# Splitting weight parts three ahead of their product instead of four, in a float32 hybrid decoder layer

## The chip, the cores and the metric

One core of one Trainium2 chip runs the whole program. The metric is device time in microseconds (us) from the start to the end of one execution; lower is better. The time of before is the median of three runs.

## What is computed

One decoder layer over 1024 positions of width 1024, in float32. Cut to what matters here:

```python
def reference(x, norm1_g, w_in, conv_w, conv_norm_g, ret_norm_g, w_out,
              norm2_g, w_up, w_down, final_norm_g):
    h = x
    h = h + hybrid_mixer(rms_norm(h, norm1_g), w_in, conv_w, conv_norm_g, ret_norm_g, w_out)
    h = h + sq_relu_mlp(rms_norm(h, norm2_g), w_up, w_down)
    return rms_norm(h, final_norm_g)

def hybrid_mixer(u, w_in, conv_w, conv_norm_g, ret_norm_g, w_out):
    z = u @ w_in                      # 1024 x 3584, columns for conv and retention
    ...                               # short convolution; chunkwise retention, 4 heads
    return jnp.concatenate([y_conv, y_ret], axis=-1) @ w_out

def sq_relu_mlp(u, w_up, w_down):
    hdn = jax.nn.relu(u @ w_up)       # 1024 x 4096
    return (hdn * hdn) @ w_down
```

## The kernel before

**Products.** Each float32 matrix is used as a sum of two fp32r parts, a rounded one and the rest, and a product is three matmul passes: high by high, high by low, low by high. The input projection, the output projection and the MLP run on TensorE (PE) in products of 12 matmuls (128x128 weights, 512 moving columns) or, in `tile_in` (L520), in pieces of 24. Many of the products are those of a seven-product (Strassen-like) scheme, numbered 1 to 7; their left sides are sums of weight blocks.

**Splitting a weight part.** `split_piece` (L168) takes one 128x512 block of weights that a DMA has brought into a tile `r`. ScalarE (ACT) copies it to `wh`, which rounds it; VectorE (DVE), or GpSimd (POOL) in the mixer when the planner finds it freer, subtracts to give `wl`. `wh` and `wl` have four buffers each (pool `wp`, L108). In the seven-product scheme `Left.split` (L209) also issues POOL operations on the raw blocks (`r<-r,r`, three of them after the part of product 2, one after that of product 5) and, for four of the seven, one DMA that fetches a later block.

**Order of the work.** Nothing reorders instructions: each engine executes its own in the order in which the program emits them, and SyncE (SP) issues the DMAs in that order as well. The list `plan` holds all splits in the order of their products. `prepare()` (L180) takes the next from the list, emits it, and appends the part to `parts`, from which a product pops its weights. How many parts are ahead is therefore settled by how often `prepare` was called before the first product: L297 and L381 call it for two parts each, and then each product pops one and calls it once. Before the output projection a planner (`background`, L428) chooses, from costs it keeps per engine, where the elementwise tasks of convolution, gates and norms go between the products. From the output projection on, the order is written out by hand.

**The stages.** (1) Head: x is loaded, scaled and split; the value projection. (2) `tile_in` pieces and `pair_in` (L824), with retention and convolution beside them. (3) Tiles 22 and 23 (`IN_END`), which use each weight part twice, for the left and the right half of the positions (L910 to L926). (4) The output projection: `group` (L1060), four groups of eight steps; steps 0 to 3 pop a part each, steps 4 to 7 use these again for the right half and call `prepare`. After its matmuls a step with c = 1 reads the bank out: a DVE add into `x` and an ACT square (`out_evac`, L995). Then the steps of `todo` follow. (5) The MLP. Its first 14 products (`for at, ...`, L1251) and then seven cycles of 28 (L1332 to L1348) have one body:

```python
            bk = pairs[x].product(y)      # or down_product
            prepare()
            for f in todo.pop(0):         # splits of activations, V; sums on POOL
                f()
            put_now()
            pairs[x].take(y, bk)          # DVE (or ACT) reads the bank
```

In a cycle, `up` products (into two banks, pool `pu`) alternate with `down` products (four banks, two for each). `take` reads a bank with one to three DVE operations (`t<-t,b`), `down_take` (L1280) with two or four (`x<-x,b`). Activations are split in `v_split` (L1192): ACT copy, then a subtraction `V<-t,V` on DVE or, for j = 1 of most products, on POOL; `v_next` (L1201) forms sums on POOL (`t<-t,t`). Tiles of `x2` that were put aside in DRAM are fetched back at the steps at = 3 and 4 (`fetch_back`, L1034, `x<-k`) and combined on POOL from at = 7 on (`new_basis`, L1004, the first `x<-x,x`). (6) The last stage multiplies what the last 512 hidden columns give (`last_mm`, L1382), with weights `wd` that `last_piece` (L1106) splits, and normalises and stores the result.

Products of the MLP are counted here from the first, product 0 (at = 0); the first cycle begins with product 14.

Of the kernel before, what the change touches and what calls it, by code (L numbers as in the profile page):

```python
# [40 lines left out]
IN_END = [22, 23]  # L41
# [38 lines left out]
def hybrid_layer(  # L80
# [51 lines left out]
    def bank(pool_=None):  # L132
        return (pool_ or pm).tile([P, H], F32, tag="b", name=nm("b"))
# [46 lines left out]
    def prepare(n=1):  # L180
        for _ in range(n):
            if plan:
                part = plan.pop(0)()
                if part is None:
                    part = plan.pop(0)()
                parts.append(part)
# [191 lines left out]
                dve.tensor_scalar_mul(to[:, h, :], src, perhead[:, i, h : h + 1])  # L378

    once = [token_norms]  # L380
    prepare(2)  # L381

    R2 = ssq

# [12 lines left out]
    def mm(piece, banks, rhs, start, stop, ks=range(4)):  # L397

        hi, lo = piece
        ops = [(a, r, k) for k in ks for a, r in ((hi, 0), (hi, 1), (lo, 0))]  # L400
        for i, (a, r, k) in enumerate(ops):
            for n, b in enumerate(banks):
                nc.tensor.matmul(  # L403
                    b, a[:, k, :], rhs(n, k)[r],
                    start=(start and i == 0), stop=(stop and i == len(ops) - 1),
                )
# [15 lines left out]
    def spawn(gen, ready=None, late=0.0):  # L422
        Task(gen, now[0] if ready is None else ready, late).go()
# [36 lines left out]
    def slot():  # L460
        now[0] += SLOT

    def force(key):
        while key not in got:
            background(1e9)
            assert key in got, key
# [36 lines left out]
    def tick(look=LOOK):  # L503
        n = -1
        while n != len(procs):
            n = len(procs)
            background(look)
            norms()
# [227 lines left out]
    def use(f, half, out, z, psum):  # L736

        if f >= 20:
            return gate(f - 20, half, z, out, psum)
        if f % 3 == 1:  # L740
            return conv_h(f // 3, half, z, psum)
        return conv_b(f // 3, half, z, out, psum)
# [168 lines left out]
    for half in range(2):  # L911
        for f, (z, banks, pieces) in ends.items():
            for c in range(2):
                if half == 0:
                    pieces.append(parts.pop(0))
                mm(
                    pieces[c], [banks[half]],
                    lambda n, k: (uh[4 * c + k][:, hs[half]], ul[4 * c + k][:, hs[half]]),
                    c == 0, c == 1,
                )  # L920
                slot()
                if half:
                    prepare()
                if c:
                    spawn(use(f, half, z, banks[half], True), clock[dve])
                tick()  # L926
# [68 lines left out]
    def out_evac(i, half, b):  # L995
        x, g = scaled(i, half)
        dve.tensor_add(x, x, b)
        square_into(sums_[half], x, i == 0)
        if i < 4:
            if un[i] is None:  # L1000
                un[i] = unit(s="un")
            act.activation(un[i][:, hs[half]], x, AF.Copy, scale=g)
# [57 lines left out]
    def group(j):  # L1060
        a, b = j, 4 + j
        ws, banks = {}, {}
        steps = [(a, 0, 0), (b, 0, 0), (a, 1, 0), (b, 1, 0), (a, 0, 1), (b, 0, 1), (a, 1, 1), (b, 1, 1)]
        for s, (i, c, half) in enumerate(steps):
            if half == 0:
                ws[i, c] = parts.pop(0)
            elif j == 0:
                for idx in range(4 * c, 4 * c + 4):
                    force(("split", idx, 1))
            if c == 0:  # L1070
                banks[i, half] = bank((pm, pr)[i == b])
            mm(
                ws[i, c], [banks[i, half]],
                lambda n, k: (y_h[4 * c + k][:, hs[half]], y_l[4 * c + k][:, hs[half]]),
                c == 0, c == 1,
            )
            slot()
            if half:
                prepare()
            if c:  # L1080
                out_evac(i, half, banks[i, half])
            for t in todo.get(8 * j + s, []):
                t()
            if s == 2 and j in (1, 2):
                down.fetch(4)
            tick()
# [8 lines left out]
    for j in range(4):  # L1095
        group(j)
# [467 lines left out]
```

## Time and profile before

| | |
|---|---|
| median of the three runs | 1070.92 us (1070.82 to 1071.99) |
| profiled execution | 1070.03 us, of which the span in the trace is 1068.1 us |
| PE busy | 1054.8 us (99%), 4860 matmuls |
| DVE / ACT / POOL busy | 870.8 (82%) / 463.6 (43%) / 561.6 us (53%) |
| chain that ended last | PE 90%, DVE 6%, ACT 2% |
| granted TensorE clock | 0.999 of full speed |

The 1.9 us between the span and the execution's own time lie around the span. In the timeline a row gives start, duration, engine, line and operation, the tiles written and read, how many instructions were merged, and in brackets the idle time of the engine before it and what ended it. A matmul row's duration is longer than the pitch of matmuls, since they overlap. L74 is the line of the helper through which all elementwise operations are emitted, so tiles tell them apart. A releaser is the one that came last by the profile; where it had long been done it was another.

### The profile page before, as it was taken

Reading aid. Unit: us, or ns where it says so; the run is one execution under the profiler, and the core shown is the slowest. Engines: PE = TensorE matmul, PEld = TensorE weight load, DVE = VectorE, ACT = ScalarE, POOL = GpSimd, SP = SyncE. Lnnn points to the kernel's source line nnn. Section 1 sums busy time; section 2 is a strip of 40 time slices with the busy share of each in tenths; the row PEclk is TensorE's granted clock in tenths of the full one; section 3 lists DMA queues with packets and bytes.
Section 4 is the critical chain, followed back from the end, with each engine's and each line's share of the span. In section 5 each row is a group of like instructions: output and inputs, shape, how many; then the busy total and the mean of one; then the engine's idle time right before and its main releaser. Section 6 shows DMA issues by size and latency. Waiting matters only on the chain.

```text
span 1068.1 us, 13853 instructions
## 1 busy us (share of the span) xinstructions
PE 1054.8 (99%) x4860; PEld 879.2 (82%) x4860; DVE 870.8 (82%) x1231; ACT 463.6 (43%) x906; POOL 561.6 (53%) x381
## 2 busy tenths in 40 slices
PE   9999999999999999999999999999999999999997
PEld 8888888788888888788788888888888888888886
DVE  7446546799998665799999989999899899899955
ACT  8211445673437444443343433343443434334453
POOL 6334324367854233559458267277186295384552
PEclk9999999999999999999999999999999999999999
DMA  7121122122223733051221211211301201200204
GB/s 276 65 58 42 38 80 70 63 95 80 69 69 129 256 115 123 11 187 39 61 59 49 79 31 50 90 30 50 99 21 50 89 21 49 90 21 19 69 30 158
DMA packets 39685, 82.25 MB, mean 77 GB/s; under 512 B 4544, under 2 KB 5696, under 8 KB 39616
## 3 DMA queue, kind: packets, MB, share of 16 engines
q1 hardware_dynamic: 39328, 80.85, 23.5%
q8 instruction: 38, 0.62, 0.2%
q10 hardware_dynamic: 288, 0.52, 0.1%
q14 instruction: 31, 0.25, 0.1%
HBM read 71.92 MB, written 9.44 MB: 76 GB/s over the span
## 4 chain that ended last, share of the span: by engine, by line
PE 90%; DVE 6%; ACT 2%; issue 1%; POOL 1%; DVEq 0%; ACTq 0%; POOLq 0%
PE b L403 55%; PE b L1277 23%; PE b L357 4%; PE b L1386 4%; DVE t L74 1%; DVE wl L74 1%; DVE x L74 1%; DVE m L74 1%; ACT h L74 1%; DVE q L74 1%; DVE V L74 1%; PE b L339 0%; PE b L595 0%; PE b L1436 0%; PE b L246 0%
## 5 line engine op out<-in xcount | busy, mean ns | idle before, releaser
L74 ACT CAST wh<-r 128x512 fp32r<-128x512 f32 x286 | 176.6, 620 | 326.4 <-PE b L403 134.4
L403 PE MATMUL b<-U,wh 128*128 128x512 f32 x1024 | 315.8, 390 | 2.0 <-DVE x L74 1.2
L74 DVE TENSOR_TENSOR wl<-r,wh 128x512 fp32r<-128x512 f32 x250 | 232.8, 933 | 89.0 <-ACT wh L74 87.8
L74 POOL TENSOR_TENSOR r<-r,r 128x512 f32<-128x512 f32 x136 | 210.2, 1548 | 114.1 <-DVE wl L74 66.1
L1277 PE MATMUL b<-V,wh 128*128 128x512 f32 x784 | 242.0, 389 | 0.7 <-POOL V L74 0.4
L403 PEld LDWEIGHTS b<-U,wh 128*128 128x128 f32 x1024 | 191.7, 188 | 43.2 <-issue 2.4
L74 DVE TENSOR_TENSOR x<-x,b 128x512 f32<-128x512 f32 (+1 forms) x312 | 195.5, 673 | 28.8 <-PE b L1386 14.3
L403 PE MATMUL b<-U,wl 128*128 128x512 f32 x512 | 199.2, 389 | 0.0
L1277 PEld LDWEIGHTS b<-V,wh 128*128 128x128 f32 x784 | 147.1, 188 | 32.4 <-POOL V L74 0.9
L74 POOL TENSOR_TENSOR t<-t,t 128x512 f32<-128x512 f32 x70 | 106.3, 1523 | 96.4 <-ACT t L74 50.4
L1277 PE MATMUL b<-V,wl 128*128 128x512 f32 x392 | 152.5, 389 | 0.0
L74 POOL TENSOR_TENSOR wl<-r,wh 128x512 fp32r<-128x512 f32 x36 | 51.4, 1432 | 119.3 <-ACT wh L74 116.5
L403 PEld LDWEIGHTS b<-U,wl 128*128 128x128 f32 x512 | 96.1, 188 | 19.9
L403 PE MATMUL b<-uh,wh 128*128 128x512 f32 x304 | 102.3, 396 | 0.0
L403 PE MATMUL b<-ul,wh 128*128 128x512 f32 x304 | 100.5, 390 | 0.0
L403 PE MATMUL b<-uh,wl 128*128 128x512 f32 x304 | 100.2, 389 | 0.0
L1277 PEld LDWEIGHTS b<-V,wl 128*128 128x128 f32 x392 | 73.6, 188 | 15.2
L74 POOL TENSOR_TENSOR V<-t,V 128x512 fp32r<-128x512 f32 x35 | 49.6, 1418 | 67.0 <-ACT V L74 67.0
L74 DVE TENSOR_TENSOR t<-t,b 128x512 f32<-128x512 f32 x112 | 75.8, 677 | 1.7 <-POOL t L74 1.2
L74 ACT ACTIVATE t<-t 128x512 f32<-128x512 f32 x64 | 40.2, 631 | 81.2 <-DVE t L74 80.5
L74 DVE TENSOR_TENSOR V<-t,V 128x512 fp32r<-128x512 f32 x63 | 70.3, 1116 | 0.0
L403 PEld LDWEIGHTS b<-uh,wl 128*128 128x128 f32 x304 | 57.0, 188 | 12.3
(177 smaller groups left out, 1431.3 us busy)
## 6 DMA issues: line engine op xcount, KB each, us to landing
r<-w_up_t SPq DMA_DIRECT2D x64, 256.0 KB, 2.6
r<-w_down_t SPq DMA_DIRECT2D x56, 256.0 KB, 2.7
r<-w_in_t SPq DMA_DIRECT2D x48, 256.0 KB, 2.7
xt<-xT SPq DMA_DIRECT2D x16, 256.0 KB, 5.4
xs<-xT SPq DMA_DIRECT2D x8, 512.0 KB, 5.0
r<-w_out_t SPq DMA_DIRECT2D x16, 256.0 KB, 2.7
x<-xT SPq DMA_DIRECT2D x8, 512.0 KB, 7.9
k<-x SPq DMA_DIRECT2D x6, 512.0 KB, 3.0
```

What stands on the lines that cost most here:

```text
L74: return f(out, *args, **kw)
L357: nc.tensor.matmul(vb[i], a[k][:, i * P : (i + 1) * P], b[k // 2][:, vs], start=(k == 0 and a is uh and b is vh), stop=(k == KT - 1 and a ...
L403: nc.tensor.matmul(b, a[:, k, :], rhs(n, k)[r], start=(start and i == 0), stop=(stop and i == len(ops) - 1),)
L1277: nc.tensor.matmul(b, a, r, start=(i == 0), stop=(i == len(ops) - 1))
L1386: nc.tensor.matmul(z, a, b, start=(k == 0 and t == 0), stop=(k == 3 and t == 2))
```

## The change

The second `prepare` of the head takes one part instead of two. In the tiles 22 and 23, which called `prepare` four times while their parts were used for the second time, it is called once after the first product and then three times; in each group of the output projection it is called after step 0 and after steps 4, 5 and 6 instead of 4, 5, 6 and 7. Otherwise each `prepare` stays where it is.

```diff
     once = [token_norms]
-    prepare(2)
+    prepare()
...
                 slot()
-                if half:
+
+                if (f, c) == (IN_END[0], 0) if half == 0 else (f, c) != (IN_END[-1], 1):
                     prepare()
...
             slot()
-            if half:
+            if s == 0 or half and s < 7:
                 prepare()
```

No other line differs, and the MLP's own calls are not touched.

## Rows read from the trace of the kernel before

**Rows 1.** Page, busy time of each engine (share of the span, instructions).

```profile
PE 1054.8 (99%) x4860; PEld 879.2 (82%) x4860; DVE 870.8 (82%) x1231; ACT 463.6 (43%) x906; POOL 561.6 (53%) x381
```

**Rows 2.** Waits of PE: total us, times, longest us; two of seven.

```profile
PE b L663 <- ACT h L74: 2.3, 5, 0.7
...
PE b L403 <- DVE x L74: 1.2, 2, 0.7
```

**Rows 3.** Timeline of PE, single rows.

```profile
436.31 0.70 PE L403 MATMUL b<-U,wh 128*128 128x512 f32 x2 [0.70 <-DVE x L74]
...
508.37 0.61 PE L403 MATMUL b<-U,wh 128*128 128x512 f32 x2
508.82 0.39 PE L403 MATMUL b<-U,wl 128*128 128x512 f32 x1
...
515.18 0.71 PE L403 MATMUL b<-U,wh 128*128 128x512 f32 x2 [0.74 <-ACT t L74]
...
675.76 0.61 PE L1277 MATMUL b<-V,wh 128*128 128x512 f32 x2
...
956.60 0.90 PE L1277 MATMUL b<-V,wh 128*128 128x512 f32 x2
...
979.50 0.50 PE L1277 MATMUL b<-V,wh 128*128 128x512 f32 x1 [0.44 <-POOL V L74]
...
1012.57 0.74 PE L1386 MATMUL b<-hid,wd 128*128 128x512 f32 x2 [0.35 <-DVE t L74]
```

**Rows 4.** Page, the costliest groups: the two halves of a split (busy, mean ns | idle before).

```profile
L74 ACT CAST wh<-r 128x512 fp32r<-128x512 f32 x286 | 176.6, 620 | 326.4 <-PE b L403 134.4
...
L74 DVE TENSOR_TENSOR wl<-r,wh 128x512 fp32r<-128x512 f32 x250 | 232.8, 933 | 89.0 <-ACT wh L74 87.8
```

**Rows 5.** Timeline of DVE at the end of the output projection.

```profile
434.32 1.24 DVE L74 TENSOR_TENSOR wl<-r,wh 128x512 fp32r<-128x512 f32 x1 [0.46 <-ACT wh L74]
435.49 0.67 DVE L74 TENSOR_TENSOR x<-x,b 128x512 f32<-128x512 f32 x1
```

**Rows 6.** Timeline of DVE in the MLP, single rows.

```profile
507.10 0.69 DVE L74 TENSOR_TENSOR t<-t,b 128x512 f32<-128x512 f32 x1 [1.18 <-POOL t L74]
...
508.43 1.70 DVE L74 TENSOR_TENSOR wl<-r,wh 128x512 fp32r<-128x512 f32 x1
...
512.44 0.68 DVE L74 TENSOR_TENSOR wl<-r,wh 128x512 fp32r<-128x512 f32 x1
...
514.36 0.68 DVE L74 TENSOR_TENSOR t<-t,b 128x512 f32<-128x512 f32 x1
...
671.36 1.72 DVE L74 TENSOR_TENSOR wl<-r,wh 128x512 fp32r<-128x512 f32 x1
...
1010.07 1.12 DVE L74 TENSOR_TENSOR wd<-r,wd 128x512 fp32r<-128x512 f32 x1
...
1011.83 0.69 DVE L74 SCALAR_TENSOR_TENSOR t<-t,b 128x512 f32<-128x512 f32 x1
```

**Rows 7.** Timeline of POOL in the MLP, single rows.

```profile
451.19 1.74 POOL L74 TENSOR_TENSOR r<-r,r 128x512 f32<-128x512 f32 x1 [1.82 <-DVE wl L74]
464.62 1.29 POOL L74 TENSOR_TENSOR x<-x,x 128x512 f32<-128x512 f32 x1 [11.69 <-DMA x<-k]
...
505.33 1.74 POOL L74 TENSOR_TENSOR t<-t,t 128x512 f32<-128x512 f32 x1
...
669.65 1.63 POOL L74 TENSOR_TENSOR r<-r,r 128x512 f32<-128x512 f32 x1 [4.21 <-issue]
671.24 1.30 POOL L74 TENSOR_TENSOR V<-t,V 128x512 fp32r<-128x512 f32 x1
...
976.45 1.29 POOL L74 TENSOR_TENSOR r<-r,r 128x512 f32<-128x512 f32 x1 [3.62 <-PE b L403]
977.69 1.75 POOL L74 TENSOR_TENSOR V<-t,V 128x512 fp32r<-128x512 f32 x1
```

**Rows 8.** Timeline of SP's queue: the first tiles fetched back.

```profile
453.37 0.86 SPq L1036 DMA_DIRECT2D x<-k  x2
```

## The prediction

> **What bounds the kernel now.** I read the page's busy shares first: PE is busy for 99% of the span [rows 1]. So only the time that PE stands still can be won, and nothing on another engine counts until PE waits for it. Next come PE's own waits: L663 in the retention waits for ACT five times, 2.3 us in all, and the products of L403 wait twice for DVE adds `x`, 1.2 us [rows 2]. Single rows of PE's timeline give the rest [rows 3]. They need a correction: two matmuls take 508.82 - 508.37 = 0.45 us, a pitch of 0.225, but one is shown with 0.39, so an idle time of a row understates the loss by 0.165. Losses after the mixer that the change could reach are then 0.70 + 0.16 = 0.86 us at 436.31, 0.90 at 515.18, 0.60 at 979.50 and 0.51 at 1012.57, and at 956.60 two matmuls take 0.90 instead of 0.61, 0.29 [rows 3]. That is 3.2 us. The retention adds 2.3 + 5 x 0.16 = 3.1 [rows 2]. Together 6.3 us, 0.6% of the time: the most that can be gained.
>
> Then I read who makes PE wait. A split is an ACT copy of 0.62 us and a DVE subtraction of 0.93 on average; ACT's copies stand behind 326 us of idle time, most of it ended by a product on PE [rows 4]. The reason is the four buffers of `wh`: with four parts ahead, the fifth split reuses the buffer of the product just issued, so ACT stands until that product ends.
>
> **The change, part by part.** Nothing is added or removed: 286 copies, their subtractions, the POOL sums and the DMAs stay [rows 4]. With three ahead, a split that stood in one step's body stands in the next one's. Its buffer is freed at the same moment as before, so no split can run earlier than it could. What changes is the order on each in-order queue: before, a body was split, sums, read-out; now the split for the same product comes after that read-out. Everything that reads a bank thus moves ahead of one subtraction, and the split itself falls back by the sums and the read-out of one step. The DMA that a split issues and the POOL sums on raw blocks fall back with it, past that step's other POOL work.
>
> *Head, tiles, pairs.* One split fewer stands ahead of the first tile; the copies no longer wait for PE. The retention's chain of small ACT and DVE operations [rows 2] keeps its place in both queues, since `prepare` is called at the same points. The planner's clocks start about one split lower, which can move a task by a slot. Between a gain of all 3.1 us and a loss of as much, I take 0, nearest to the unchanged order. Tiles 22 and 23 and the groups keep a part for every pop; I take 0 there, as no row of PE waits for a split.
>
> *End of the output projection.* Step 7 of the last group loses its split. Its DVE add `x` at 435.49 stood behind the subtraction at 434.32 (1.24 us, plus 0.46 waiting for the copy) [rows 5]; without it the add can start 1.17 us earlier, 0.3 more than the 0.86 us that PE lost there. Product 1 then does not wait: -0.86, bounds 0 and -0.86. The wait of product 0 for the add of step 6 stays, as that step keeps its split.
>
> *First cycle.* Here that gain meets another limit. The read-out at 507.10 stands idle for 1.18 us until POOL's sum from 505.33 ends at 507.07 [rows 6, 7]: its output takes a buffer that the sum reads. POOL's string began at 464.62, held 11.69 us by the DMA that brings x2 back [rows 7]. The operations ahead of that sum are the same before and after, so I leave 507.07 unchanged. But DVE comes to this point with one subtraction less behind it, so the subtraction for product 26, done earlier before, now takes the row at 508.43 and ends at 510.13 [rows 6]. Product 26 started at 508.37 [rows 3], now 0.86 earlier, at 507.51; its third matmul, at 507.96, is the first to read `wl` and waits 2.17. Product 27 follows at 507.51 + 12 x 0.225 + 2.17 = 512.38; its subtraction takes the row at 512.44 and ends at 513.12, against 512.83 wanted: 0.29. Product 28 starts at 515.4. Before, it started at 515.18, held by the last read of its bank, 514.36 to 515.04 [rows 3, 6]. So at product 28 the gain of 0.86 and the stalls before are paid back to within 0.2.
>
> What sets the start of POOL's string is not in the trace of before as the change will have it. The fetch of `x<-k` is issued at 453.37, just after the POOL sum of 451.19 + 1.74 = 452.93 let the DMA ahead of it go [rows 7, 8]; that sum waits for a subtraction that falls back. Its cost lies between 0 (the steps before run earlier too, since product 0's split no longer waits behind the add of step 7) and one sum, 1.74. From the other side, sums that now come ahead of the raw-block ones can save up to the 1.18 us of DVE's idle time. I take -0.3 for all of this, near the middle, so 0.1 gained up to product 28; bounds -0.86 - 0.90 = -1.8 and 0.2 + 1.74 = +1.9.
>
> *Steady cycles 2 to 6.* PE loses nothing between the rows at 515.18 and 956.60 [rows 3]; nothing to gain. The cover of a split that falls back is its lead; rival three says what happens where it goes.
>
> *Last up-and-down cycle.* At 979.50 PE waits for POOL's `V`, 977.69 + 1.75 = 979.44, which stands behind the third sum of a burst, 976.45 [rows 3, 7]. The burst belongs to a split that moves past this `V`, so `V` comes first: -0.60, bounds 0 and -0.60. At 956.60 the second half of `V` on DVE comes late; one subtraction less stands ahead: -0.29, or 0. At 1012.57 the bank waits for the DVE operation of 1011.83 + 0.69, and a subtraction `wd` of 1.12 us stands before its step [rows 6]; one fewer does: -0.51, or 0. The `wd` parts are wanted one product each later and are not late.
>
> **Sum.** -0.1 - 0.60 - 0.29 - 0.51 = -1.5 us against the profiled execution's own 1070.03 (span 1068.1, and 1.9 around it), which is 0.9 below the median of the runs. From the median: 1070.92 - 1.5 = 1069.4 us. A measurement of this kernel can tell about 0.2%, 2.1 us, from no change; so I forecast a small gain that lies inside it.
>
> **The rivals.**
> 1. *More comes free (faster).* If POOL's string runs ahead by the 1.18 us, the 0.86 of the projection stays and the 0.90 at product 28 goes too: -0.86 - 0.90 - 0.60 - 0.29 - 0.51 = -3.2, 1067.7 us. For it: DVE has one subtraction less ahead of each read-out, everywhere. Against: the sum that holds DVE at 507.10 has the same work ahead of it [rows 6, 7].
> 2. *Nothing happens.* The buffers free a split at the same moment, so four ahead may never have been more than three and a wait: 1070.9 us. Against: the order on the queues does change, and the stall at 979.50 is one of order.
> 3. *A wait that is now hidden returns in every cycle (slower).* In the second half of a cycle POOL's burst waits for a subtraction before it, and `V` for the odd half follows on POOL: 669.65 + 1.63, then `V` to 672.54 [rows 7]. The subtraction falls back to the slot before the row at 671.36 [rows 6]; then the sum ends at 673.0 and `V` at 674.3. The product that starts at 675.76 reads it with its fourth matmul, 676.4 [rows 3]. 2.1 us are left. If the subtraction ends with that row instead, at 673.08, only 0.4 is left, and a `V` of 1.75 as at 977.69 instead of 1.30 [rows 7] uses that up. From there on each us costs 1 us in each of six cycles: 0.8 us late gives 4.8 - 1.5 = +3.3, 1074.2 us. For it: subtractions take 0.68 us at 512.44 and 1.72 at 671.36, where POOL is at work [rows 6], so one bad meeting costs 1.04. Against: two of them are needed.
>
> The Trainium skill, "SBUF — State Buffer", section "Who interferes with whom", says that a VectorE operation with two inputs in SBUF and a GpSimd operation that reads SBUF shut each other out: whichever comes second is blocked until the first ends. By that rule a moved subtraction that starts just behind a POOL sum loses up to a whole sum and not 1.04, and rival three would need only one such meeting. The trace agrees with the direction (0.68 against 1.72); it does not show a whole sum lost.
>
> **How the numbers follow.** The forecast has 0.48, the first rival 0.32, the second 0.08, the third 0.12. Faster by over 0.2%: the first rival nearly whole and a tail of the forecast, 0.36. Slower by over 0.2%: the third and a little of the first cycle's upper bound, 0.13. Within: 0.51. The range goes down to 1067.7 less 0.9 of the retention's 3.1, 1066.8, and up to the first cycle's bound, 1069.4 + 2.0, and part of the third rival, 1072.4.
>
> **What would show it.** Right: ACT's copies no longer idle behind PE; no PE wait at the first product 1 of the MLP, none for `V` in the last cycle; in the first cycle waits of `wl` at products 26 and 27 in place of the bank's at 28. Wrong: a PE wait in the pairs or in each steady cycle, or a retention whose waits differ from 2.3 us by more than 1 us; or product 28 earlier or later by over 1 us, after the starts are set equal at product 0.

## The result, and the profile after

The changed kernel takes 1074.13 us (median of 18 runs, 1072.13 to 1077.56), the kernel before on the same chip 1071.08 (18 runs, 1070.46 to 1072.20): a ratio of 1.0033, 95% interval [1.0025, 1.0040], 3.5 us slower by this ratio of the means (the medians differ by 3.05). 1069.4 was forecast, with a range that ended at 1072.4; slower by over 0.2% had a chance of 0.13. The profiled execution has a span of 1071.3 us against 1068.1. The profiled execution of one experiment (e12) was disturbed: it took 4990 us, with matmuls mostly 0.8 to 1.3 us apart where 0.227 is usual and no low granted clock in the profile (so not the half clock that the text for e13 gives); of that run only the ten other times are used, and e13 is its kernel again, for a trace.

The page of after, the busy times and the two halves of a split, which answer to [rows 1, 4]:

```profile
PE 1055.6 (99%) x4860; PEld 880.5 (82%) x4860; DVE 865.3 (81%) x1233; ACT 462.1 (43%) x906; POOL 557.7 (52%) x379
...
L74 ACT CAST wh<-r 128x512 fp32r<-128x512 f32 x286 | 175.0, 619 | 233.4 <-PE b L403 133.6
L74 DVE TENSOR_TENSOR wl<-r,wh 128x512 fp32r<-128x512 f32 x247 | 222.6, 903 | 53.1 <-ACT wh L74 53.0
```

The work is the same; by the planner's choice some tasks changed engine, and DVE has 247 of the subtractions instead of 250, POOL the others. What differs is who makes PE wait (after: total us, times, longest), which answers to [rows 2]:

```profile
PE b L403 <- DVE wl L74: 3.6, 2, 2.1
PE b L663 <- ACT h L74: 2.2, 5, 0.8
...
PE b L403 <- DVE t L74: 1.0, 1, 1.0
PE b L403 <- DVE x L74: 0.5, 1, 0.5
```

The retention's waits are the same (2.2 for 2.3). The waits for `V`, for the bank at product 28 and at product 1 are gone. Two waits for `wl`, which before had none, are the first row; the wait for the bank (`t`, 1.0) at product 26 is new too. The timeline of PE in after shows both, and what follows the first (single rows, as [rows 3]):

```profile
260.64 0.61 PE L403 MATMUL b<-U,wh 128*128 128x512 f32 x2
263.31 0.50 PE L403 MATMUL b<-U,wl 128*128 128x512 f32 x1 [2.06 <-DVE wl L74]
...
264.31 0.63 PE L403 MATMUL b<-U,wl 128*128 128x512 f32 x1
264.74 1.05 PE L403 MATMUL b<-U,wh 128*128 128x512 f32 x2
...
267.30 0.39 PE L403 MATMUL b<-uh,wh 128*128 128x512 f32 x1
...
512.23 0.70 PE L403 MATMUL b<-U,wh 128*128 128x512 f32 x2 [0.96 <-DVE t L74]
514.43 0.50 PE L403 MATMUL b<-U,wl 128*128 128x512 f32 x1 [1.50 <-DVE wl L74]
...
519.82 0.39 PE L403 MATMUL b<-U,wh 128*128 128x512 f32 x1
...
982.98 0.62 PE L1278 MATMUL b<-V,wh 128*128 128x512 f32 x2
```

The first wait is in the second of the `pair_in` pairs, tiles (6, 7), in the product that the code numbers n = 6. Behind it the pitch from one matmul to the next is 264.74 - 264.31 = 0.43 us, where 0.227 is usual: ten matmuls from 263.31 to 267.30 take 3.99 us instead of 2.27, so 1.7 us are lost after the wait is over. The windows view of after shows what the clock did there (window, its length, busy us and count of PE, PEld, DVE, ACT and POOL, then the granted clock, the DMA share and GB/s):

```profile
260.80:263.30 2.50, 0.45 (x3) 0.03 (x1) 2.50 (x3) 0.62 (x1) 2.42 (x3) 1.00 0.00 0
263.40:264.00 0.60, 0.60 (x3) 0.50 (x4) 0.60 (x1) 0.00 (x0) 0.60 (x1) 0.90 0.00 0
264.00:267.50 3.50, 3.50 (x10) 2.72 (x9) 3.47 (x4) 1.77 (x3) 3.29 (x3) 0.53 0.55 180
267.50:268.50 1.00, 1.00 (x6) 0.79 (x5) 1.00 (x2) 0.14 (x1) 0.28 (x1) 1.00 0.45 158
```

PE had stood for 2.06 us; then the granted clock fell to about half for most of the third window (1.2 instead of 2.4 GHz), and came back.

To see where time went, take the start of the same PE matmul in both traces and subtract (after less before). This offset, in us:

| | after | e1 | e3 | e5 | e6 | e9 | e11 | e13 | e8 |
|---|---|---|---|---|---|---|---|---|---|
| at 256, two products ahead of the late one | -0.2 | 0.0 | -0.4 | -0.2 | +0.7 | -0.2 | -0.5 | +0.4 | +0.7 |
| product 0 of the MLP | +4.0 | 0.0 | +3.2 | +2.4 | +3.2 | +3.1 | +2.5 | +0.5 | +0.7 |
| product 1 | +3.2 | -0.9 | +2.3 | +1.6 | +2.3 | +2.2 | +1.7 | +0.5 | +0.7 |
| product 28 | +4.6 | +1.7 | +6.9 | +4.5 | +4.1 | +4.7 | +4.7 | +1.0 | +1.2 |
| before the last cycle (900) | +4.6 | +1.6 | +6.8 | +4.4 | +4.1 | +4.6 | +4.6 | +1.0 | +1.2 |
| after it (1025) | +2.9 | -0.2 | +5.0 | +2.6 | +2.3 | +2.9 | +2.8 | -0.8 | -0.6 |

The first line scatters by up to 0.7 either way: e8, whose program is that of before up to there, has +0.7. It says nothing of the change. For after: 4.1 us are lost in the pairs (all of it by 268, and nothing more up to product 0), 0.8 gained at product 1 and 1.5 lost up to product 28, nothing changes in the steady cycles, and 1.7 are gained in the last cycle. (In e5 the ten extra matmuls are skipped in the pairing; their 2.27 us are in the offset.) The lines from product 28 on need care: the traces of e1, e5, e9 and e11 have one stretch of 3.4 us at the low clock in the first cycle, 1.7 us each, and e3 has one twice as long; after, e6, e13 and e8 have none there.

### The profile page after: what moved, and what is told of

It reads as the page before. It is cut to its first block, busy times and chain, and to the rows that moved or that the text cites. A ratio compares the mean times of both kernels' runs of the same rounds, so it can differ in the third digit from the quotient of the medians.

```text
span 1071.3 us, 13763 instructions
## 1 busy us (share of the span) xinstructions
PE 1055.6 (99%) x4860; PEld 880.5 (82%) x4860; DVE 865.3 (81%) x1233; ACT 462.1 (43%) x906; POOL 557.7 (52%) x379
## 4 chain that ended last, share of the span: by engine, by line
PE 86%; DVE 4%; POOL 4%; ACT 3%; issue 2%; DMA 0%; SPq 0%; DVEq 0%; POOLq 0%; ACTq 0%
PE b L403 52%; PE b L1278 23%; PE b L357 4%; PE b L1387 4%; POOL r L74 2%; ACT h L74 1%; DVE m L74 1%; POOL t L74 1%; DVE q L74 1%; POOL x L74 1%; DVE wl L74 0%; PE b L339 0%; POOL a L74 0%; ACT U L74 0%; DVE h L74 0%
## 5 line engine op out<-in xcount | busy, mean ns | idle before, releaser
L403 PE MATMUL b<-U,wh 128*128 128x512 f32 x1024 | 316.8, 391 | 1.4 <-DVE t L74 1.0
L74 DVE TENSOR_TENSOR wl<-r,wh 128x512 fp32r<-128x512 f32 x247 | 222.6, 903 | 53.1 <-ACT wh L74 53.0
L1278 PE MATMUL b<-V,wh 128*128 128x512 f32 x784 | 241.4, 389 | 0.0
L403 PEld LDWEIGHTS b<-U,wh 128*128 128x128 f32 x1024 | 192.6, 188 | 42.0 <-issue 2.2
L403 PE MATMUL b<-U,wl 128*128 128x512 f32 x512 | 200.2, 391 | 3.6 <-DVE wl L74 3.6
L1278 PEld LDWEIGHTS b<-V,wh 128*128 128x128 f32 x784 | 147.2, 188 | 30.5
L1278 PE MATMUL b<-V,wl 128*128 128x512 f32 x392 | 152.7, 389 | 0.0
L74 POOL TENSOR_TENSOR wl<-r,wh 128x512 fp32r<-128x512 f32 x39 | 56.4, 1448 | 123.4 <-ACT wh L74 104.8
L403 PEld LDWEIGHTS b<-U,wl 128*128 128x128 f32 x512 | 96.5, 188 | 24.6 <-DVE wl L74 4.7
L403 PE MATMUL b<-uh,wh 128*128 128x512 f32 x304 | 102.3, 396 | 0.0
L403 PE MATMUL b<-ul,wh 128*128 128x512 f32 x304 | 100.4, 390 | 0.0
L403 PE MATMUL b<-uh,wl 128*128 128x512 f32 x304 | 100.2, 389 | 0.0
L1278 PEld LDWEIGHTS b<-V,wl 128*128 128x128 f32 x392 | 73.7, 188 | 15.8 <-DVE wl L74 0.6
L74 DVE TENSOR_TENSOR V<-t,V 128x512 fp32r<-128x512 f32 x63 | 75.6, 1200 | 0.1
L403 PEld LDWEIGHTS b<-ul,wh 128*128 128x128 f32 x304 | 57.1, 188 | 12.3
```

What stands on the lines that cost most here:

```text
L74: return f(out, *args, **kw)
L403: nc.tensor.matmul(b, a[:, k, :], rhs(n, k)[r], start=(start and i == 0), stop=(stop and i == len(ops) - 1),)
L1278: nc.tensor.matmul(b, a, r, start=(i == 0), stop=(i == len(ops) - 1))
```

## Experiments

Gains and losses below are the ratio less 1, times 1071 us, with its interval.

**In which stage is the time lost? (e1, e2)** First three ahead only from the output projection on (e1), then only up to the tiles 22 and 23, where one `prepare` more makes it four again (e2).

```diff
e1, against before (L1078)
-            if half:
+            if (s == 0 and j) or (half and s < 7):
                 prepare()
e2, against after (L923, L1079)
-                if (f, c) == (IN_END[0], 0) if half == 0 else (f, c) != (IN_END[-1], 1):
+                if half or (f, c) == (IN_END[0], 0):
                     prepare()
...
-            if s == 0 or half and s < 7:
+            if half:
                 prepare()
```

> Four ahead through the mixer, three from the output projection on. Theory A (the loss is made in the pairs, by 3.9 us, and the rest of the change gains 0.8 + 0.3 - 1.8 + 0.2 + 0.7 + 0.8 = 1.0): 1.0 us below the kernel before of this comparison, between -0.5 and -1.8, and no wait of PE for wl in the pairs. Rival B (the offsets between the two profiles mislead, and what costs is the first cycle): +2 to +3 us, as the change itself.

> Three ahead through the mixer, four from tiles 22 and 23 on, so the output projection and the MLP are as before. Theory A: the pairs cost as in the changed kernel, +3.5 to +4.5 us against the kernel before, with one wait of about 2 us for wl in the second pair and a stretch of low granted clock behind it. Rival B: within 0.5 us of the kernel before.

e1: 1070.89 us, ratio 0.9994 [0.9985, 1.0003], -0.6 us [-1.6, +0.3]. e2: 1074.99 us, 1.0037 [1.0024, 1.0050], +4.0 us [+2.6, +5.4]. Both as theory A has it: the mixer makes the whole loss, and the rest of the change is a gain too small to be told from nothing. In e2 the same wait of 2.1 us stands in the same product, with the low clock behind it. In e1 the pairs are as before, and a low clock showed in the first cycle instead (e1, timeline of PE):

```profile
507.94 0.70 PE L403 MATMUL b<-U,wh 128*128 128x512 f32 x2 [0.69 <-DVE t L74]
510.14 0.50 PE L403 MATMUL b<-U,wl 128*128 128x512 f32 x1 [1.49 <-DVE wl L74]
510.47 1.01 PE L403 MATMUL b<-U,wh 128*128 128x512 f32 x2
```

Ten matmuls from 510.14 on take 3.98 us. In after the same place had waits of 0.96 and 1.50 and kept its clock: 22 matmuls in 519.82 - 514.43 = 5.39 us, where 22 at 0.227 make 4.99, and a granted clock of 1.00 from 514.5 to 519.8. So e1's trace contains 1.7 us that come in some executions only: five of its eleven have a mean granted clock of 0.996 and a median of 1071.3 us, the six others (0.998 and 0.999) 1070.0.

**Does the low clock follow the wait? (e5)** PE gets something to do while it would wait.

```diff
     def product(n, bank_, extra=0):
         b = bank(bank_)
+        for _ in range(extra):
+            nc.tensor.matmul(b, parts[0][0][:, 0, :], U[name][0][0], start=True, stop=True)
         mm(parts.pop(0), ...)
...
-            b = product(n, (pm, pr)[at % 2])
+            b = product(n, (pm, pr)[at % 2], 10 if (fs, n) == ((6, 7), 6) else 0)
```

> The changed kernel with ten extra matmuls of 512 columns (2.27 us at 0.227 each) ahead of the late product of the second pair, into the bank that the product then begins anew, so that PE works while the subtraction is awaited. Their results are thrown away. Theory C (the low granted clock follows PE's standing still): no wait of 2 us and no stretch at a pitch of 0.427 in the pairs; from the second pair on the offset to the kernel before is +2.0 to +2.6 instead of +3.9, and the whole is 1.2 to 2 us faster than the changed kernel, about +1.5 us against the kernel before. Rival D (the low clock has another cause at this place, the pairs' load): the stretch stays, and the time is that of the changed kernel, +3.1 us, or above.

1072.88 us, 1.0016 [1.0007, 1.0025], +1.7 us: half of the loss of after, with the subtraction as late as there. Windows of e5, and PE's row of the extra matmuls:

```profile
260.80:263.30 2.50, 2.50 (x13) 1.91 (x11) 2.50 (x3) 0.62 (x1) 2.42 (x3) 1.00 0.00 0
264.00:267.50 3.50, 3.50 (x17) 2.87 (x16) 3.47 (x4) 1.78 (x3) 3.29 (x3) 1.00 0.57 167
```

```profile
260.52 2.43 PE L783 MATMUL b<-U,wh 128*128 128x512 f32 x10
262.78 0.62 PE L403 MATMUL b<-U,wh 128*128 128x512 f32 x2
```

The clock stays at 1.00 in the stretch where after has 0.53, under the same load on DVE and POOL, so theory C's signs came and rival D's did not. Of after's loss in the pairs about 2.3 us is the wait, and 1.7 the low clock behind it.

**Is it the shorter lead, or the planner's other choices? (e3, e4)** With three ahead the planner's clocks differ, and it puts some tasks at other steps and on other engines. Its choices were written down for both kernels (`PLACES`, which task at which call; `SPLITS`, the engine of each subtraction) and replayed in the other one.

```diff
     def tick(look=LOOK):
-        n = -1
-        while n != len(procs):
-            n = len(procs)
-            background(look)
-            norms()
+        for step in places.pop(0):
+            if step == 'N':
+                norms()
+            else:
+                eng = {'a': act, 'd': dve, 'p': pool, 'n': None}[step[-1]]
+                tasks[int(step[:-1])].go(eng)
```

> The changed kernel, but the planner's choices (which elementwise task goes at which step on which engine, and which engine subtracts for wl) are those of the kernel before, written down and replayed. Theory A1 (the wait in the pairs comes from the choices, which put two more conv tasks on POOL ahead of the raw-block sums): the wait is gone or under 0.5 us, and the time is 0.5 to 1.5 us below the kernel before. Rival A2 (the shorter lead alone makes the wait): the wait in the second pair stays at 1.5 to 2.5 us, and the time is +2.5 to +3.5 us.

> The kernel before with four ahead everywhere, but with the planner's choices of the changed kernel replayed. If the choices alone make the wait: +3 to +4 us with a wait for wl in the second pair. If it takes the choices and the shorter lead together (a product is 2.7 us, the wait 2.1): no wait in the pairs, within 0.5 us of the kernel before. If the shorter lead alone makes it: also within 0.5 us, but then the replay of the old choices at three ahead still waits.

e3: 1074.35 us, 1.0028 [1.0017, 1.0040], +3.0 us. e4: 1071.32 us, 0.9999 [0.9991, 1.0008], no difference, and no wait in the pairs. Theory A1 falls: with the old choices the wait only moves, to a product 2.7 us later (1.26 us) and to the next pair (0.3 and smaller ones), 3.6 us in all between 256 and product 0. A2's time came; its wait is smaller than the 1.5 it named. With e4, which has the new choices and no loss, the lead makes the loss; the choices say where it shows.

**Which queue holds the late subtraction? (e6, e9, e11)** In after the subtraction for the late product is the first of the two in the last row here (after, timelines of ACT, POOL and DVE):

```profile
254.59 0.72 ACT L74 ACTIVATE cv<-a,sm 128x512 f32<-128x512 f32 x1 [5.88 <-POOL a L74]
256.30 0.62 ACT L74 CAST wh<-r 128x512 fp32r<-128x512 f32 x1 [0.98 <-POOL r L74]
257.67 0.62 ACT L74 CAST wh<-r 128x512 fp32r<-128x512 f32 x1 [0.76 <-POOL r L74]
```

```profile
251.12 1.73 POOL L74 TENSOR_TENSOR a<-a,z 128x512 f32<-128x512 f32 x1
252.94 1.62 POOL L74 TENSOR_TENSOR a<-a,ssq 128x512 f32<-128x512 f32 x1
254.52 6.52 POOL L74 TENSOR_TENSOR r<-r,r 128x512 f32<-128x512 f32 x4
```

```profile
258.71 2.88 DVE L74 SCALAR_TENSOR_TENSOR cv<-a,sm,cv 128x512 f32<-128x512 f32 x2
261.51 3.43 DVE L74 TENSOR_TENSOR wl<-r,wh 128x512 fp32r<-128x512 f32 x2
```

Three things stand in front: POOL's raw-block sums behind two multiplications of `a`, ACT's copies behind a `cv` copy that waits for these, and DVE's two `cv` operations. Three runs moved one each, all with the choices of after replayed: e6 the first two sums, e9 the whole convolution half, e11 the `cv` copy besides.

```diff
e6
-            if n == (1 if self.five_first else 2):
+            if n == (1 if self.five_first or self.stream is mix else 2):
                 pool.tensor_add(a21, a21, a22)
-            if n == 2:
+            if n == (1 if self.stream is mix else 2):
                 pool.tensor_sub(a11, a21, a11)
+            if n == 2:
                 pool.tensor_sub(a12, a12, a11)
e9, in PLACES: task 19 is conv_h(1, 1); calls 66, 71, 76, 77
-18d 19p 19p 19n N N | ... | 19a N | ... | 19d N N | 20p 20n N
+18d N N | ... | 19p 19p 19n N | ... | 19a N N | 19d 20p 20n N
e11, on top of e9
-        act.activation(cv[:, sl], a[:, sl], AF.Copy, scale=w[2])
+        if (i, half) != (1, 1):
+            act.activation(cv[:, sl], a[:, sl], AF.Copy, scale=w[2])
         yield (dve,)
+        if (i, half) == (1, 1):
+            dve.tensor_scalar_mul(cv[:, sl], a[:, sl], w[2])
```

> The changed kernel with its planner's choices replayed; in the pairs alone POOL's first two sums on raw blocks are issued one part earlier, after the split for product 1. Theory E (the late subtraction comes from these sums, which stand one product later on POOL's queue): the copy for the late product no longer waits for POOL, the 2.1 us wait in the second pair goes below 0.7, no low clock there, and the time is +0 against the kernel before (-1 to +0.7). Rival F (DVE's own string of z, cv and cv ahead of the subtraction sets it): the wait stays between 1.5 and 2.5, +2.5 to +3.5 us.

> The changed kernel with its planner's choices replayed, except that the four steps of one convolution half (the two multiplications of a on POOL, the cv copy on ACT, the cv operations on DVE) are each issued one product later, so that they stand behind the same split as before the change. Theory J (the split that fell back one product now stands behind these tasks, on POOL for the raw-block sums and on ACT for the copy; the order alone makes the wait): the raw-block sums end before 256, the copy for the late product starts before 256, PE's wait of 2.1 us in the second pair falls below 0.5 and no low clock follows there; the time is -0.5 to +0.5 us against the kernel before. Rival K (DVE has too much work in this stretch whatever the order): a wait of 1 us or more stays in the second or third pair, +1.5 to +3 us.

> As the run with one convolution half issued one product later, and in addition the cv copy of that half (a times a per-partition weight) runs on DVE, just ahead of DVE's own two cv operations, instead of on ACT. Theory N (ACT's in-order queue makes the wait: the copy for the late product stands behind a cv copy that waits for POOL's multiplications; 5.1 us of ACT's idle time there): no copy in this stretch idles over 3 us, PE's waits in the second pair (0.8 and 1.2 us) fall below 0.4 together, and at the first MLP product the offset to the kernel before is +0.3 to +1.0 instead of +2.2 to +2.5; 1 to 2 us faster than the run without this edit. Rival O (DVE has too much work in this stretch, and 0.7 us more makes it worse): waits of 1.5 us or more stay in the second pair, same time or slower.

e6: 1073.77 us, 1.0021 [1.0012, 1.0029], +2.2 us; e9: 1074.57, 1.0030 [1.0019, 1.0042], +3.2; e11: 1074.50, 1.0033 [1.0021, 1.0045], +3.5. Each moved what it meant to move, and none won what its theory promised. e6: the copies stood behind the same `cv` copy, now for 9.49 us, and PE waited 0.3 and 1.2 us. e9: the first copy went early, the next one stood behind the `cv` copy, and PE waited 0.6 and 1.0 us. e11: no copy is held there any more, and PE waits at the next product instead, 1.11 us. In e9 and e11 PE also waits 0.5 us for a POOL subtraction two pairs later. The timelines of ACT, first e9, then e11:

```profile
254.26 0.62 ACT L74 CAST wh<-r 128x512 fp32r<-128x512 f32 x1 [5.57 <-POOL r L74]
259.97 0.73 ACT L74 ACTIVATE cv<-a,sm 128x512 f32<-128x512 f32 x1 [5.09 <-POOL a L74]
260.60 0.60 ACT L74 CAST wh<-r 128x512 fp32r<-128x512 f32 x1
```

```profile
253.81 0.62 ACT L74 CAST wh<-r 128x512 fp32r<-128x512 f32 x1 [5.57 <-POOL r L74]
255.19 0.62 ACT L74 CAST wh<-r 128x512 fp32r<-128x512 f32 x1 [0.75 <-POOL r L74]
```

And the timeline of DVE in e11, with the subtraction that is now late at its end:

```profile
259.96 1.50 DVE L74 TENSOR_SCALAR cv<-a,sm 128x512 f32<-128x512 f32 x1 [2.56 <-POOL a L74]
261.50 2.45 DVE L74 SCALAR_TENSOR_TENSOR cv<-a,sm,cv 128x512 f32<-128x512 f32 x2
263.87 0.68 DVE L74 TENSOR_TENSOR wl<-r,wh 128x512 fp32r<-128x512 f32 x1
```

Between 256 and product 0 they lose 2.5 (e6), 3.2 (e9) and 3.0 us (e11), all without a low clock there. Theory N is right for the one product and wrong for the sum: in these runs the task that waits for POOL's `a` held the queue that it stood in, ACT's for 9.49 and 5.09 us, DVE's for 2.56, and one product fewer of lead is one product fewer to hide that. In e4 a `cv` copy stands idle for 5.84 us with two copies of splits behind it, and PE does not wait. Whether some order of all three queues would fit three ahead was not tried.

**The first cycle (e7, e12, e13).** Four ahead again for the first cycle with three ahead at products 1 to 13 (e7), and the reverse, three from the cycle's first product on (e12, and e13, the same kernel).

```diff
e7, against before
-            if half:
+            if half and (j, s) != (3, 7):
                 prepare()
...
-        prepare()
+        prepare(2 if at == 13 else 1)
...
-            prepare()
+            if (b, at) != (1, 0):
+                prepare()
e12 and e13, against before
-        prepare()
+        if at != 13:
+            prepare()
```

> Four ahead through the mixer and up to the last step of the output projection, three for the first 13 products of the MLP, four again for the first cycle (one part more at product 13), three from the second cycle on. Theory G (the first cycle's cost is the subtraction for product 26 that falls behind a read-out): no wait for wl in the first cycle; the 0.8 of product 1 is spent on waiting for the bank at product 28 again, and the last cycle gains 0.2 + 0.7 + 0.7 = 1.6: -1.6 us against the kernel before, between -0.8 and -2.8. Rival H (the gain at product 1 is what makes the first cycle late, not the order): a wait of over 1 us for wl in the first cycle, -0.5 to +1.5.

> Four ahead up to the end of the first 14 MLP products, three from the first product of the first cycle on. Theory P (the first cycle's cost is made before it: the POOL sum that fell back at products 4 to 6 held the DMA ahead of the x2 fetches, so that POOL's string started 1.4 us later): the string starts as in the kernel before, and the first cycle loses less than 0.7 more than before; -1.0 to -2.0 us against the kernel before, the last cycle's gains included. Rival Q (it is the order within the cycle: the subtraction for product 26 behind the read-out that waits for POOL): wl waits of 1 us or more at products 26 or 27, and -0.5 to +1.0 us.

> The same kernel as in the run before (three ahead from the first product of the first cycle on), for a trace that can be read: that one's profiled execution was taken at 4990 us, with PE at half clock throughout. Theory P: POOL's string starts as in the kernel before, no wait for wl of 1 us or more at products 26 and 27, and the offset at product 28 is within 0.7 of that at product 0. Rival Q: waits for wl of 1 us or more at products 26 or 27. Time as in the ten undisturbed executions of that run, 1069.2 to 1070.7.

e7: 1069.81 us, 0.9986 [0.9977, 0.9994], -1.5 us. e12: 1070.34, 0.9989 [0.9980, 0.9998]; e13: 1070.29, 0.9990 [0.9981, 1.0000]; both about -1.1 us. The timelines of POOL, first e1 and then e13, show the two ways in which the cycle can lose, to be read beside [rows 7]:

```profile
452.98 1.68 POOL L74 TENSOR_TENSOR r<-r,r 128x512 f32<-128x512 f32 x1 [1.95 <-DVE wl L74]
466.04 1.50 POOL L74 TENSOR_TENSOR x<-x,x 128x512 f32<-128x512 f32 x1 [11.38 <-DMA x<-k]
```

```profile
451.69 1.74 POOL L74 TENSOR_TENSOR r<-r,r 128x512 f32<-128x512 f32 x1 [1.83 <-DVE wl L74]
465.66 1.84 POOL L74 TENSOR_TENSOR x<-x,x 128x512 f32<-128x512 f32 x1 [12.24 <-DMA x<-k]
```

With three ahead at products 1 to 13 (e1) the raw-block sum is at 452.98 against 451.19 while the products are 0.87 earlier: 2.7 us later in the order of the products, one whole product; the x2 fetches behind it and POOL's string start 2.3 us later so. That is the step that theory P names.

With the string nearly in time (e13, +0.5) PE still waits 1.52 us for `wl` at product 26, since the subtraction stands behind the read-out that waits for POOL. That is Q's sign, and P's "no such wait" is wrong. But the time is P's (-1.1 us): the wait takes the place of the bank's waits at products 27 and 28, and product 28 is only 0.5 later than product 0.

e7 has the order of before and a late string. G's signs came: no wait for `wl`, and -1.5 us; H's wait for `wl` did not. But the gain at product 1 is more than spent, 1.45 us from product 1 to product 28, where G allowed for 0.8, and the loss is made at product 22 (e7, PE):

```profile
498.25 0.70 PE L403 MATMUL b<-U,wh 128*128 128x512 f32 x2 [1.11 <-DVE t L74]
```

So a late string alone can lose what after loses there (1.5), and the order alone 0.5. The two do not add up; how much of after's 1.5 belongs to each is not shown. e7's -1.5 us in all is the last cycle's.

**The part that pays, alone (e8), and a fetch moved (e10).**

```diff
e8, against before; at counts the products of cycle b
-            prepare()
+            if (b, at) != (1, 0):
+                prepare()
e10, on top of e8
-        call(sum4, 3) + lo("t3", dve, 3) + hi("t4", 3) + call(fetch_back, 0, 1),
-        lo("t4", dve, 3) + call(fetch_back, 2, 4, 5, 6),
+        call(sum4, 3) + lo("t3", dve, 3) + hi("t4", 3),
+        lo("t4", dve, 3),
...
+        for i in {3: (0, 1), 4: (2, 4, 5, 6)}.get(at, ()):
+            fetch_back(i)
         prepare()
```

> Four ahead up to the end of the first cycle, three from the second cycle on, and nothing else. Theory: up to the second cycle as the kernel before; the last cycle's three waits shrink by 0.2, 0.7 and 0.7 as in the changed kernel, no new wait in cycles 2 to 6: -1.6 us against the kernel before, between -1.0 and -2.0. Rival: those three shrank in the changed kernel because everything before them had been delayed by 4.5 us, not because of the lead: 0, between -0.5 and +0.5.

> Four ahead through the first cycle, three from the second cycle on (-1.8 us against the kernel before when measured without this edit), and the x2 tiles are fetched back ahead of the split of their step instead of behind it. Theory L (the first cycle's remaining waits come from POOL's string, which starts when the fetched tiles land, and the fetches stand on SP's queue behind weight DMAs that wait for POOL's raw-block sums): the fetches are issued 1.5 to 3 us earlier, POOL's first sum on x2 starts 1 to 3 us earlier, the waits at products 22, 26 and 28 (0.6, 0.4 and 0.9 us) shrink, and the time is -2.3 to -3.7 us against the kernel before. Rival M (the string is bound by work ahead of it on POOL or by buffers, not by the fetch): the waits stay, -1.3 to -2.2 us.

e8: 1069.48 us, 0.9982 [0.9973, 0.9991], -1.9 us [-2.9, -1.0], faster than both kernels. The three waits of the last cycle are gone, as in after (e8, PE; the first row belongs to the first wait, the next two to the second, the last to the third):

```profile
957.10 0.62 PE L1277 MATMUL b<-V,wh 128*128 128x512 f32 x2
...
978.86 0.62 PE L1277 MATMUL b<-V,wh 128*128 128x512 f32 x2
...
979.54 0.62 PE L1277 MATMUL b<-V,wh 128*128 128x512 f32 x2
...
1011.50 1.75 PE L1387 MATMUL b<-hid,wd 128*128 128x512 f32 x7
```

From 900 to 1025 it gains 1.17 + 0.57 = 1.74 us, as after does (4.62 - 2.88 = 1.74), so the delay in front, 4.6 us there and 1.2 here, has no part in it: theory and time agree, and the rival falls. e10: 1069.23 us, 0.9980 [0.9971, 0.9989], not to be told from e8. Theory L falls: four of the six fetches are issued some 2 us earlier, and POOL's first sum starts no earlier (465.29 against 464.62 in before, with the products 0.5 later). The last of the six tiles lands at 465.16 (464.49 in before), in both 0.13 us ahead of the sum, and in e1, e7, e8 and e13 the sum follows its tile as closely. So it still waits for the tile, though the profile of e10 names a product on PE that ended 0.07 us after the landing; rival M's time came, its reason (work or buffers in front) is not shown. In the order of the products the last tile lands only 0.3 us sooner than in e8. The windows view of e10 fits that: from 458 on the DMA engines are full (the share is the last figure but one).

```profile
458.00:462.00 4.00, 4.00 (x26) 3.53 (x26) 3.93 (x10) 1.08 (x2) 0.00 (x0) 1.00 1.02 401
462.00:466.00 4.00, 4.00 (x22) 3.36 (x21) 3.12 (x6) 0.98 (x2) 0.71 (x1) 1.00 1.03 399
```

## Why the prediction was wrong

**The step that failed is "Head, tiles, pairs": 0.** It cost 4.1 us. The reason given was "nearest to the unchanged order", between bounds of 3.1 either way that were worked out from the retention's waits; these did not move (2.2 us in five waits, as forecast). For the tiles and groups the text adds that no row of PE waits for a split. Both look at whether PE waits now, and not at how much time was left before it would. The trace of before has what should have been read, first on DVE and then on PE:

```profile
255.74 1.72 DVE L74 TENSOR_TENSOR wl<-r,wh 128x512 fp32r<-128x512 f32 x1
```

```profile
261.11 0.39 PE L403 MATMUL b<-U,wl 128*128 128x512 f32 x1
```

The subtraction of the product that came late ends at 255.74 + 1.72 = 257.46 and is first read at 261.11: a cover of 3.65 us. In after it starts at 261.51 and ends, with the same kind of duration, just ahead of the matmul that waited for it, 263.3. It fell back 5.8 us, one product (2.7) and 3.1 of other work, so 2.1 are missing, the wait of 2.06. "The split itself falls back by the sums and the read-out of one step" was true of the hand-written part; in the mixer a step's queue also holds the planner's tasks, with waits of their own. Rival three had this mechanism, a hidden wait that returns behind POOL, but in the MLP's cycles. Nor did the bounds help: the loss of up to 3.1 is not among the terms of the stated range, and no bound had the 1.7 us of the clock.

The cover alone does not pick this product. Two products later it was smaller, 266.55 - 263.17 = 3.38 us (before, DVE and PE):

```profile
262.49 0.68 DVE L74 TENSOR_TENSOR wl<-r,wh 128x512 fp32r<-128x512 f32 x1
```

```profile
266.55 0.39 PE L403 MATMUL b<-U,wl 128*128 128x512 f32 x1
```

That subtraction fell back by 2.9 us only (in after it is on POOL and ends at 266.10) and would have been in time. What counts is the cover less what the part falls back.

**End of the projection: -0.86.** Right: 0.83, and the wait at product 0 stays at 0.5.

**First cycle: -0.1 up to product 28.** The mechanism was right, the size off. The wait came at product 26 as forecast (2.17 was worked out for `wl`; it is 0.96 for the bank and 1.50 for `wl`), and the bank's wait at 28 is gone. From product 0 to 28 after loses 0.7 instead of gaining 0.1. The mis-sized term is "I take -0.3 for all of this", which came out near +0.5: the sum that lets the fetch go fell back a whole product. POOL's string starts at 470.53 in after against 464.62, 2.8 us later once the 3.1 of the products are taken off, where the text allowed 1.74.

**Steady cycles: 0.** Right; the offset is the same at 515 and at 900. Rival three's wait did not come.

**Last cycle: -0.60, -0.29, -0.51.** Right: 0.70, 0.28 and 0.63, with some small ones 1.7 instead of 1.4; e8 has it alone.

**What would show it.** "ACT's copies no longer idle behind PE" was wrong: they still idle 134 us behind the products of L403 (134 before) and 40 behind those of L1278 (L1277 before, 121; [rows 4] shows L403 alone). The fall comes from copies that now stand behind other work of ACT, not from earlier ones: of the 141 copies in the steady cycles one starts over 0.1 us earlier against the products, 86 start within 0.1, 54 later. A copy takes the buffer of the part four products back in either kernel, as the prediction itself had said. The sign of being wrong, a PE wait in the pairs, is what happened.

The parts after the mixer add up to 0.65 - 1.74 = -1.1 from product 0, where -1.5 was forecast, and e1, which is these parts alone, measures -0.6 [-1.6, +0.3]. The error is the pairs.

The Trainium skill ("TensorE: Matmul & The Clock Gate", section "Architectural detail: the array is 16× 32×32, not 1× 128×128") calls ACT and DVE strict FIFO queues. The trace agrees: in e9 the copy at 260.60, whose raw-block sum was done at 255.60, stood behind a `cv` copy that idled 5.09 us.

## What to carry to other kernels

That nobody waits for a part now does not say how long it can be late. Before taking lead away, work out for each part the time between the end of its preparation and its first use, and set against it what the step that it moves to holds in every queue that it uses, waits included. Where buffers already set when work can start, as here, lead only sets what stands in front of it. So shorten it stage by stage, keep what pays (here from the second cycle on, -1.9 us), and leave the lead where bursts of other work share the queues (here the pairs). Moving the blockers one at a time moved the wait and kept most of the loss.

## What was not expected of the hardware

A wait of 2.06 us in an otherwise busy PE was followed by some 3.5 us at a granted clock of about half, which cost 1.7 us more; with PE kept busy (e5) the clock stayed. The other trace with a wait of 2.1 us, e2, has the same stretch. With shorter waits it came in some traces and not in others. At product 26, waits of 0.96 and 1.50 us close to each other left the clock at full speed in after, and 1.20 and 1.49 in e6, while 0.69 and 1.49 at the same place in e1 did not. In the pairs of e3, e6, e9 and e11 waits of 1.0 to 1.3 us (in e6 and e9 with one of 0.3 and 0.6 ahead) were followed by none. What decides it is not shown.

It also widens the spread: of the 18 executions of after the five with a mean granted clock of 0.999 took 1072.1 to 1074.1 us, the five with 0.993 took 1076.6 to 1077.6. One stretch of 3.4 us at half clock lowers the mean by 0.0016, so the five at 0.999 had none or hardly any; their median, 1072.9, is still 1.8 us above before. So the low clock makes a good part of the 3.5 us, and not all of it.
